# High halves of the weights on GpSimd in the three norm stretches of a layer, on the scalar engine elsewhere

## The chip, the core and the metric

The kernel runs on one core of a Trainium2. Its engines work side by side, each through its own queue in order: TensorE (PE) multiplies, VectorE (DVE), ScalarE (ACT) and GpSimd (POOL) work on elements, and SyncE (SP) starts the transfers between device memory and on-chip memory. A semaphore makes an instruction wait for one of another engine. SBUF is the on-chip memory of operands, PSUM that of TensorE's results. The metric is the time of one execution on the device in microseconds, as the median of three runs, without a profile.

## What is computed

A decoder of two layers, 1024 rows (tokens) of 1024 numbers, all fp32. In each layer the normed rows go through one input projection into three groups of heads, their outputs through an output projection; then a gated MLP with 2816 channels and a short convolution follows. Each of the two parts has a norm before and a norm behind it. Cut to what matters here:

```python
def rms_norm(x, gain, eps=NORM_EPS):
    xf = x.astype(jnp.float32)
    y = xf * lax.rsqrt(jnp.mean(xf * xf, axis=-1, keepdims=True) + eps)
    return (y * gain.astype(jnp.float32)).astype(x.dtype)
...
        h = rms_norm(x, pre_mix_norm[layer])
        proj = h @ w_in[layer]
...
        mix = jnp.concatenate([o_diff, o_dil, o_ssd], axis=-1) @ w_out[layer]
        x = x + rms_norm(mix, post_mix_norm[layer])
        h = rms_norm(x, pre_ffn_norm[layer])
        u = causal_dwconv(h @ ffn_up[layer], ffn_conv_w[layer], ffn_conv_b[layer])
        g, val = jnp.split(u, [D_FF], axis=-1)
        f = (jax.nn.silu(g) * val) @ ffn_down[layer]
        x = x + rms_norm(f, post_ffn_norm[layer])
```

## The kernel before

**Split products.** Every product with weights is made of three products of TensorE in its fast fp32r format. `wsplit` (L139) loads a tile of weights (fp32, buffer `wr`), rounds it to its high half `wh` on ScalarE, and subtracts that on VectorE, which leaves the low half `wl`; both are in line 154:

```python
A.activation(h, r, AF.Copy), V.tensor_tensor(part(lo), r, fr(h), op=ALU.subtract)
```

Activations are split in the same way into `ah` and `al` (or `g`, for the hidden channels). A product adds up wh·ah, wl·ah and wh·al in PSUM: L170, L173 and L174 in `tm3` (rows stand on the partitions, as for the values, the output and the down projection), L230, L233 and L234 in `mm3` (channels stand on the partitions, as for the up projection). `wr` has three buffers, `wh` and `wl` four. A tile of weights has 1024 elements on each of 128 partitions; the last of a down group has 512, those of the values' projection have 768 (two rows of 384) or 2x262.

**Rows and halves.** The 1024 rows are eight tiles of 128, worked on in two halves T=0 and T=1 of four tiles. A half goes through the mixer while the other is in the dense products: `weave` and `follow` take the next step of one Python generator between the steps of another, and a tile scheduler puts each engine's instructions in order by priority and by what they need, and sets the waits. So an edit of one operation can also move its neighbours in the order of an engine.

**A norm.** For each row tile: the square summed along the row on ScalarE (L836 for the output projection, L906 for the down projection, L273 for the second norm, 1.06 us of a row of 1024), mean and constant on VectorE (L113, L117), the power -1/2 on GpSimd (L116, one element on each partition), one step of refinement on VectorE (L119, L120), then row times scale times gain (L308) and the sum with the residual row (L309), both on VectorE. The next layer part's norm follows: square (L273), L113, L117, L116, L119, L120 and the scaled row `P` (L278). TensorE transposes that row (L288, eight squares of 128), ScalarE makes the high half of it (L291) and VectorE the low half (L292).

```python
i = V.tensor_scalar(m[:, :n], ssq, scale, eps, op0=ALU.mult, op1=ALU.add)
...
G.tensor_tensor(r[:, :n], m[:, :n], mhalf[:, :n], op=ALU.pow)
```

**Where a norm is made.** In three stretches of a layer, with dense work laid beside it by `follow`, which gives a number of steps of the dense generator ahead of each transposed row tile:

- A: behind the output projection of half 0 (`out_units(0, pair)`), beside the rest of the values' projection of half 1 (`tm1`, L1012): four tiles of 2x262 and four of 768. The first pair of the up projection (two tiles of 1024) comes behind.
- B: behind the output projection of half 1 (`out_units(1, pair)`), beside the last down group of half 0 (`down_group(0, NG - 1, fT0)`, L1033): tiles of 1024, 512, 1024, 512. VectorE adds each result of it to the sum so far (L884, one input in PSUM). The first pair of the up projection of half 1 comes behind.
- C: in layer 1, beside the values' projection of half 0 (`tm_in(0)`, L995): twelve tiles; the norm is that of the rows which layer 0 ended with.

`up_pair` (L842) makes one pair of the up projection: two tiles of weights, the convolution, the gate (L860, L864). L749 is a scaling on GpSimd in the attention of the mixer, L815 one of VectorE with its input in PSUM. `quiet` and the other names of the change are in the section on it.

Of the kernel before, what the change touches and what calls it, by code (L numbers as in the profile page):

```python
# [13 lines left out]
AF = mybir.ActivationFunctionType  # L14
# [55 lines left out]
def body(ctx, tc, x_in, win, wva, wvb, wvz, wout, wup, wdn, cst, gains, dtb, alog, lamp, kst, rope, out):  # L70
# [34 lines left out]
    def fr(ap):  # L105
        return ap.bitcast(F32)
# [20 lines left out]
    xsrc = [x_in[t] for t in range(8)]  # L127

    ahead = [None, None]
    lastdma = [None]  # L130

    def queue_behind(ins, before):
# [4 lines left out]
    def wsplit(src, step=None):  # L137

        raw = sp.tile([P, KT * P], F32, tag="wr", bufs=3, name="wr")  # L139
        hi = sp.tile([P, KT * P], F32R, tag="wh", bufs=4, name="wh")  # L140
        lo = sp.tile([P, KT * P], F32R, tag="wl", bufs=4, name="wl")
        n = src.shape[-1]
        step = step or n

        def part(t):
            if len(src.shape) == 2:
                return t[:, :n]
            k = src.shape[1]
            if n == step:
                return t[:, :k * n]  # L150
            return t[:, :k * step].rearrange("p (a n) -> p a n", a=k)[:, :, :n]
        r, h = part(raw), part(hi)
        lastdma[0] = Y.dma_start(r if n < step else raw[:, :r.shape[-1]].rearrange("p (a n) -> p a n", n=n) if len(src.shape) == 3 else r, src)
        for i, b in zip((A.activation(h, r, AF.Copy), V.tensor_tensor(part(lo), r, fr(h), op=ALU.subtract)), ahead):  # L154
            if b is not None:
                queue_behind(i, b)
        return hi, lo
# [177 lines left out]
    for l in range(NL):  # L335
# [583 lines left out]
        def ffn(T, pair, fT):  # L919
            for gi, (k0, n) in enumerate(GROUPS):  # L920
                for j in range(k0, k0 + n):
                    yield from up_pair(T, j, pair)
                if gi < len(GROUPS) - 2:
                    yield from down_group(T, gi, fT)

# [10 lines left out]
        if l == 0:  # L936
            hT[0] = act_pair()
            xs = [t4()]
            Y.dma_start(xs[0][:], xsrc[0])
            g0 = sp.tile([P, DM], F32, tag="gb", bufs=2, name="gb")  # L940
            Y.dma_start(g0[:], gains[l, 0])
            Y.dma_start(kc[:, 0:K_TRI], kst[:, 0:K_TRI])
            zero = t2("cv", 4)
            V.memset(zero[:], 0.0)
            wz = tr()
            for _ in range(3):
                T_.matmul(wz[:], zero[:, :P], zero[:], start=True, stop=True)
            rs = [rows() for _ in range(4)]
            done = [pre_a(0, xs[0], rs[0], g0, True)]
            ahead[1] = done[0]  # L950

            def before(t):
                if t == -2:
                    ahead[:] = pre_b(0, rs[0], hT[0])
                if t == -4:
                    xs.extend(load_x(0, 1, 2))
                if t < 0:
                    return
                if t:
                    last = pre_b(t, rs[t], hT[0])  # L960
                if t == 3:
                    done[0] = last[0]
                if t < 3:
                    done.append(pre_a(t + 1, xs[t + 1], rs[t + 1], g0, False, done[t]))
                if t == 0:
                    late[0] = lastdma[0]
                    xs.extend(load_x(0, 2))
                    ahead[:] = None, None
            dense = tm_in(0, before)
            for t in range(4):  # L970
                next(dense)
            load(kc[:, K_TRI:K_MD], kst[:, K_TRI:K_MD])
            gt0 = t2("cv", 4)
            load(gt0[:, :P], kst[:, K_GT:])
            V.tensor_copy(gtr[:, :P], gt0[:, :P])
            cs, sw, fw, sm, nA, nlam = layer_constants()
            for t in range(4):
                next(dense)
            load(kc[:, K_MD:], kst[:, K_MD:K_GT])
            hT[1] = act_pair()  # L980
            xs = load_x(1)
            rs1 = [rows() for _ in range(4)]
            ahead[0] = done[0]
            for t in range(4):
                pre_a(4 + t, xs[t], rs1[t], g0)
            ahead[0] = None
            for t in range(4):
                next(dense, None)
                with tc.high_priority(), tc.issue_after(lastmm[0].ins):
                    pre_b(4 + t, rs1[t], hT[1])  # L990
            run(dense)
        else:
            cs, sw, fw, sm, nA, nlam = layer_constants()
            hT[0] = nextT
            dense = tm_in(0)  # L995
            hT[1] = follow(dense, 1, fin1, (3, 1, 1, 1))
            run(dense)
        dt_sums(0)
        run(units(DILC, (0,)))
        mix0 = chain(attn(0, DILH), attn(0, DIFH))  # L1000
# [8 lines left out]
        run(mix0)  # L1009
        run(dense)  # L1010
        hold[0] = lastmm[0]
        hp = follow(tm1, 0, rs, (0, 1, 1, 1))  # L1012
        run(tm1)
        hold[0] = None
# [15 lines left out]
        dense, rs = out_units(1, pair)  # L1030
        run(dense)
        hold[0] = lastmm[0]
        dense = down_group(0, NG - 1, fT0)  # L1033
        hp = follow(dense, 1, rs, (1, 2, 2, 3))
        run(dense)
# [101 lines left out]
```

## Time and profile before

| what | value |
| --- | --- |
| median of 3 runs | 2664.93 us (2664.46 to 2665.4) |
| time of the profiled execution | 2661.19 us |
| span of the profile | 2659.4 us |
| TensorE busy | 2606.3 us, 98% |
| VectorE busy | 1832.2 us, 69% |
| ScalarE busy | 1246.6 us, 47% |
| GpSimd busy | 229.9 us, 9%, 228 instructions |
| conversions to a high half on ScalarE | 406 instructions, 406.3 us |
| low halves on VectorE | 406 instructions, 477.8 us |
| granted clock of TensorE | 0.996 of full speed |

The span goes from the first to the last instruction in the profile; the profiled execution's own time lies 1.8 us above it, and the median of the runs 3.7 us above that. Busy times are sums over the whole span: a share says how full an engine is on the mean, not where another waits for it. What the span has beside TensorE's busy time is 53.1 us, in which TensorE waits or starts.

### The profile page before, as it was taken

What the parts mean: (1) busy time and instruction counts of PE and PEld (TensorE: products, weight loads), DVE (VectorE), ACT (ScalarE), POOL (GpSimd) and SP (SyncE); (2) the same over time, 40 slices, a digit from 0 to 9 for tenths busy, and PEclk for the clock granted to TensorE, in tenths of its full rate; (3) what the DMA queues carried; (4) which work ended last, traced back from release to release, by engine and by line L of the source; (5) the groups of instructions that cost most, each with busy time, mean ns of one, the idle gap of its engine ahead of it and who ended that gap; (6) DMA issues with size and microseconds to landing.
All of it is one profiled execution on the core that took longest, in us unless ns stands there. A gap on an engine that the chain in (4) does not pass through costs nothing.

```text
span 2659.4 us, 37090 instructions
## 1 busy us (share of the span) xinstructions
PE 2606.3 (98%) x13454; PEld 2160.4 (81%) x13454; DVE 1832.2 (69%) x3855; ACT 1246.6 (47%) x2179; POOL 229.9 (9%) x228
## 2 busy tenths in 40 slices
PE   8999999999999999999999999999999999999998
PEld 7887878887788877888888878788877888788886
DVE  6668856567878586666765688565688775956666
ACT  4465444555534454333344564455565344543332
POOL 0100310110002010000002013101100110100001
PEclk9999999999999999999999999999999999999999
DMA  6654645344433454233257545444434334633332
GB/s 234 220 171 142 209 143 167 115 113 124 139 95 116 122 200 145 95 96 96 88 173 230 162 151 196 144 149 122 121 113 138 97 111 131 233 96 95 97 98 68
DMA packets 163720, 368.92 MB, mean 139 GB/s; under 512 B 18257, under 2 KB 64209, under 8 KB 163537
## 3 DMA queue, kind: packets, MB, share of 16 engines
q1 hardware_dynamic: 163536, 366.54, 44.1%
q8 instruction: 107, 1.75, 0.3%
q14 instruction: 77, 0.62, 0.1%
HBM read 306.18 MB, written 60.29 MB: 138 GB/s over the span
## 4 chain that ended last, share of the span: by engine, by line
PE 80%; DVE 10%; ACT 3%; issue 3%; DMA 2%; POOL 1%; SPq 0%; ACTq 0%; DVEq 0%; POOLq 0%
PE acc L230 16%; PE acc L234 15%; PE acc L233 15%; PE acc L174 7%; PE acc L170 7%; PE acc L173 7%; PE po L781 3%; PE s L631 3%; PE tr L771 3%; DVE wl L154 1%; POOL rs_r L116 1%; DVE cv L395 1%; DVE P L278 1%; DVE P L308 1%; DVE t L309 1%
## 5 line engine op out<-in xcount | busy, mean ns | idle before, releaser
L230 PE MATMUL acc<-ah,wh 128*128 128x512 f32 x1952 | 775.4, 398 | 0.5 <-ACT ah L291 0.5
L234 PE MATMUL acc<-ah,wl 128*128 128x512 f32 x1952 | 764.9, 392 | 0.0
L233 PE MATMUL acc<-al,wh 128*128 128x512 f32 x1952 | 764.5, 392 | 0.0
L154 DVE TENSOR_TENSOR wl<-wr,wh 128x1024 fp32r<-128x1024 f32 (+3 forms) x406 | 477.8, 1182 | 270.6 <-ACT wh L154 263.9
L154 ACT ACTIVATE wh<-wr 128x1024 fp32r<-128x1024 f32 (+3 forms) x406 | 406.3, 1008 | 465.5 <-PE acc L233 262.6
L230 PEld LDWEIGHTS acc<-ah,wh 128*128 128x128 f32 x1952 | 366.6, 188 | 80.5 <-issue 9.3
L234 PEld LDWEIGHTS acc<-ah,wl 128*128 128x128 f32 x1952 | 366.6, 188 | 78.1 <-issue 2.4
L233 PEld LDWEIGHTS acc<-al,wh 128*128 128x128 f32 x1952 | 367.0, 188 | 71.4 <-DVE al L292 0.8
L395 DVE SCALAR_TENSOR_TENSOR cv<-acc,cs,cv 128x511 f32<-128x511 f32 (+2 forms) x436 | 324.5, 744 | 17.8 <-ACT cv L393 15.8
L170 PE MATMUL acc<-wh,g 128*128 128x512 f32 x704 | 280.3, 399 | 3.8 <-DVE cv L401 1.8
L173 PE MATMUL acc<-wl,g 128*128 128x512 f32 x704 | 276.1, 392 | 3.0 <-DVE wl L154 3.0
L174 PE MATMUL acc<-wh,g 128*128 128x512 f32 x704 | 275.7, 394 | 1.6 <-DVE g L864 1.6
L173 PE MATMUL acc<-wl,ah 128*128 128x512 f32 (+2 forms) x640 | 226.0, 354 | 7.1 <-DVE wl L154 6.4
L170 PE MATMUL acc<-wh,ah 128*128 128x512 f32 (+2 forms) x640 | 224.1, 354 | 6.7 <-ACT wh L154 6.2
L636 ACT ACTIVATE P<-P,tiny 128x128 f32<-128x128 f32 (+7 forms) x224 | 173.0, 773 | 115.0 <-DVE tiny L635 109.6
L174 PE MATMUL acc<-wh,al 128*128 128x512 f32 (+2 forms) x640 | 223.7, 351 | 0.4 <-DVE al L292 0.2
L633 DVE CUSTOM_DVE_ANT_0 P<-s,kc 128x512 f32<-128x512 f32 (+3 forms) x224 | 129.7, 588 | 109.0 <-PE s L631 107.5
L116 POOL TENSOR_TENSOR rs_r<-rs_m,kc 128x1 f32<-128x1 f32 (+2 forms) x88 | 71.2, 813 | 1397.8 <-DVE rs L117 1256.2
L170 PEld LDWEIGHTS acc<-wh,g 128*128 128x128 f32 x704 | 132.5, 188 | 38.7 <-ACT g L863 4.3
L393 ACT ACTIVATE cv<-acc,cs 128x512 f32<-128x512 f32 x204 | 155.7, 763 | 13.8 <-PE acc L234 13.3
L174 PEld LDWEIGHTS acc<-wh,g 128*128 128x128 f32 x704 | 132.4, 188 | 32.9 <-DVE g L864 5.6
L173 PEld LDWEIGHTS acc<-wl,g 128*128 128x128 f32 x704 | 132.6, 188 | 29.3 <-DVE wl L154 4.0
(176 smaller groups left out, 3138.3 us busy)
## 6 DMA issues: line engine op xcount, KB each, us to landing
wr<-in_wup SPq DMA_DIRECT2D x176, 512.0 KB, 3.5
wr<-in_wdn SPq DMA_DIRECT2D x80, 512.0 KB, 3.5
wr<-in_win SPq DMA_DIRECT2D x54, 512.0 KB, 5.2
wr<-in_wout SPq DMA_DIRECT2D x32, 512.0 KB, 4.3
xd<-t SPq DMA_DIRECT2D x24, 512.0 KB, 2.6
t<-xd SPq DMA_DIRECT2D x24, 512.0 KB, 3.8
t<-in_x SPq DMA_DIRECT2D x16, 512.0 KB, 4.9
Q<-DQ SPq DMA_DIRECT2D x128, 64.0 KB, 2.0
```

The costliest lines, as they stand in the source:

```text
L116: G.tensor_tensor(r[:, :n], m[:, :n], mhalf[:, :n], op=ALU.pow)
L154: for i, b in zip((A.activation(h, r, AF.Copy), V.tensor_tensor(part(lo), r, fr(h), op=ALU.subtract)), ahead):
L170: i = T_.matmul(a, xh, hi[:, w], start=(n0 + k == 0), stop=False)
L173: T_.matmul(a, xh, lo[:, w], start=False, stop=False)
L174: lastmm[0] = T_.matmul(a, xl, hi[:, w], start=False, stop=(n0 + k == n - 1))
L230: i = T_.matmul(a[:], hi[:, w], xh, start=(k == 0), stop=False)
L233: T_.matmul(a[:], hi[:, w], xl, start=False, stop=False)
L234: i = T_.matmul(a[:], lo[:, w], xh, start=False, stop=(k == nk - 1))
L393: A.activation(u[:], a[:], AF.Identity, scale=w[:, n:n + 1], bias=w[:, taps:taps + 1])
L395: V.scalar_tensor_tensor(u[:, d:], a[:, :H - d], w[:, n - d:n - d + 1], u[:, d:], op0=ALU.mult, op1=ALU.add)
L633: V.tensor_tensor_reduce(p[:, c:c + n], s[:, :n], mask[:, o:o + n], 1.0, -1e30 if c == 0 else mx[:, e], ALU.add, ALU.max, mx[:, e])
L636: A.activation(p[:, :nk * P], p[:, :nk * P], AF.Exp, scale=scale, bias=nm[:, e], accum_out=den[:, e])
```

## The change

A flag `quiet` is set ahead of C, A and B and cleared at the end of C and after the first pair of an `ffn`. While it is set, `wsplit` rounds the high half by a GpSimd instruction (times 1.0 plus 0.0) in place of ScalarE's copy. 44 tiles are moved: 10 in each A (four of 2x262, four of 768, two of 1024), 6 in each B (1024, 512, 1024, 512, 1024, 1024) and 12 in C (four of 768, four of 2x262, four of 768). The low halves stay on VectorE.

```diff
--- before.py
+++ after.py
@@ -127,6 +127,7 @@
     xsrc = [x_in[t] for t in range(8)]
 
     ahead = [None, None]
+    quiet = [False]
     lastdma = [None]
 
     def queue_behind(ins, before):
@@ -151,7 +152,8 @@
             return t[:, :k * step].rearrange("p (a n) -> p a n", a=k)[:, :, :n]
         r, h = part(raw), part(hi)
         lastdma[0] = Y.dma_start(r if n < step else raw[:, :r.shape[-1]].rearrange("p (a n) -> p a n", n=n) if len(src.shape) == 3 else r, src)
-        for i, b in zip((A.activation(h, r, AF.Copy), V.tensor_tensor(part(lo), r, fr(h), op=ALU.subtract)), ahead):
+        up = A.activation(h, r, AF.Copy) if not quiet[0] else G.tensor_scalar(h, r, 1.0, 0.0, op0=ALU.mult, op1=ALU.add)
+        for i, b in zip((up, V.tensor_tensor(part(lo), r, fr(h), op=ALU.subtract)), ahead):
             if b is not None:
                 queue_behind(i, b)
         return hi, lo
@@ -920,6 +922,7 @@
             for gi, (k0, n) in enumerate(GROUPS):
                 for j in range(k0, k0 + n):
                     yield from up_pair(T, j, pair)
+                    quiet[0] = False
                 if gi < len(GROUPS) - 2:
                     yield from down_group(T, gi, fT)
 
@@ -992,9 +995,11 @@
         else:
             cs, sw, fw, sm, nA, nlam = layer_constants()
             hT[0] = nextT
+            quiet[0] = True
             dense = tm_in(0)
             hT[1] = follow(dense, 1, fin1, (3, 1, 1, 1))
             run(dense)
+            quiet[0] = False
         dt_sums(0)
         run(units(DILC, (0,)))
         mix0 = chain(attn(0, DILH), attn(0, DIFH))
@@ -1009,6 +1014,7 @@
         run(mix0)
         run(dense)
         hold[0] = lastmm[0]
+        quiet[0] = True
         hp = follow(tm1, 0, rs, (0, 1, 1, 1))
         run(tm1)
         hold[0] = None
@@ -1030,6 +1036,7 @@
         dense, rs = out_units(1, pair)
         run(dense)
         hold[0] = lastmm[0]
+        quiet[0] = True
         dense = down_group(0, NG - 1, fT0)
         hp = follow(dense, 1, rs, (1, 2, 2, 3))
         run(dense)
```

In the changed kernel every line number is higher by 1 or 2 from L130 on: the conversion is L155, the low half L156, L170/L173/L174 are L172/L175/L176, L278 is L280, L288 is L290, L292 is L294 and L884 is L886; L113 to L120 keep theirs. The scheduler's order moves with the edit. Here are the places that the prediction speaks of.

The queue of GpSimd in B of layer 0 before the change: `rs_r` are the powers, two for each of the four row tiles.

```order
```order
L116 TENSOR_TENSOR rs_r_8960<-rs_m_8959,kc_69 128x1
L116 TENSOR_TENSOR rs_r_8975<-rs_m_8974,kc_69 128x1
L116 TENSOR_TENSOR rs_r_9013<-rs_m_9012,kc_69 128x1
L116 TENSOR_TENSOR rs_r_9028<-rs_m_9027,kc_69 128x1
L116 TENSOR_TENSOR rs_r_9066<-rs_m_9065,kc_69 128x1
L116 TENSOR_TENSOR rs_r_9081<-rs_m_9080,kc_69 128x1
L116 TENSOR_TENSOR rs_r_9119<-rs_m_9118,kc_69 128x1
L116 TENSOR_TENSOR rs_r_9134<-rs_m_9133,kc_69 128x1
```


The same queue after the change, from the second row tile on; `wh` are the high halves.

```order
```order
L116 TENSOR_TENSOR rs_r_9013<-rs_m_9012,kc_69 128x1
L116 TENSOR_TENSOR rs_r_9028<-rs_m_9027,kc_69 128x1
L155 TENSOR_SCALAR wh_9144<-wr_9143 128x1024
L155 TENSOR_SCALAR wh_9150<-wr_9149 128x512
L155 TENSOR_SCALAR wh_9230<-wr_9229 128x1024
L116 TENSOR_TENSOR rs_r_9066<-rs_m_9065,kc_69 128x1
L155 TENSOR_SCALAR wh_9236<-wr_9235 128x512
L116 TENSOR_TENSOR rs_r_9081<-rs_m_9080,kc_69 128x1
L116 TENSOR_TENSOR rs_r_9119<-rs_m_9118,kc_69 128x1
L155 TENSOR_SCALAR wh_9315<-wr_9314 128x1024
L155 TENSOR_SCALAR wh_9355<-wr_9354 128x1024
L116 TENSOR_TENSOR rs_r_9134<-rs_m_9133,kc_69 128x1
```


The six conversions now stand between the powers: three ahead of the first power of the third row tile (`rs_r_9066`), one ahead of its second, two ahead of the last power.

VectorE at the end of B in layer 0, before the change, from the last add of the down group's first results to the low halves of the last normed row tile; `P_8895` is that row, `wl_9316` and `wl_9356` are the low halves of the up projection's first pair.

```order
```order
L884 TENSOR_TENSOR fT_4394<-acc_9266,fT_4394 128x512
L119 SCALAR_TENSOR_TENSOR rs_q_9136<-rs_r_9134,rs_2_9135 128x1
L154 TENSOR_TENSOR wl_9316<-wr_9314,wh_9315 128x1024
L120 SCALAR_TENSOR_TENSOR rs_r_9134<-rs_q_9136,rs_r_9134 128x1
L884 TENSOR_TENSOR fT_4394<-acc_9277,fT_4394 128x512
L278 SCALAR_TENSOR_TENSOR P_8895<-t4_8905,rs_r_9134,gb_8757 128x1024
L884 TENSOR_TENSOR fT_4394<-acc_9288,fT_4394 128x512
L154 TENSOR_TENSOR wl_9356<-wr_9354,wh_9355 128x1024
L292 TENSOR_TENSOR al_9167<-tr_9299,ah_9166 128x4x128
L292 TENSOR_TENSOR al_9167<-tr_9306,ah_9166 128x4x128
```


The same place after the change.

```order
```order
L886 TENSOR_TENSOR fT_4394<-acc_9241,fT_4394 128x512
L119 SCALAR_TENSOR_TENSOR rs_q_9136<-rs_r_9134,rs_2_9135 128x1
L886 TENSOR_TENSOR fT_4394<-acc_9266,fT_4394 128x512
L120 SCALAR_TENSOR_TENSOR rs_r_9134<-rs_q_9136,rs_r_9134 128x1
L156 TENSOR_TENSOR wl_9316<-wr_9314,wh_9315 128x1024
L280 SCALAR_TENSOR_TENSOR P_8895<-t4_8905,rs_r_9134,gb_8757 128x1024
L886 TENSOR_TENSOR fT_4394<-acc_9277,fT_4394 128x512
L886 TENSOR_TENSOR fT_4394<-acc_9288,fT_4394 128x512
L156 TENSOR_TENSOR wl_9356<-wr_9354,wh_9355 128x1024
L294 TENSOR_TENSOR al_9167<-tr_9299,ah_9166 128x4x128
L294 TENSOR_TENSOR al_9167<-tr_9306,ah_9166 128x4x128
```


One L886 has moved from ahead of the scaled row (L280) to behind it, and L120 has moved from behind the first low half to ahead of it.

TensorE at the end of A in layer 0, before the change: `acc_4225` is the last sum of the 2x262 tiles, `tr_4211` and `tr_4218` the last transposed row tile.

```order
```order
L170 MATMUL acc_4225<-wh_4091,ah_547 128x262
L173 MATMUL acc_4225<-wl_4092,ah_547 128x262
L174 MATMUL acc_4225<-wh_4091,al_548 128x262
L288 MATMUL tr_4211<-kc_69,P_3808 128x128 x4
L288 MATMUL tr_4218<-kc_69,P_3808 128x128 x4
L170 MATMUL acc_4278<-wh_4255,ah_547 128x384
```


The same place after the change.

```order
```order
L176 MATMUL acc_4225<-wh_4085,al_548 128x262
L290 MATMUL tr_4211<-kc_69,P_3808 128x128 x4
L290 MATMUL tr_4218<-kc_69,P_3808 128x128 x4
L172 MATMUL acc_4225<-wh_4085,ah_547 128x262
L175 MATMUL acc_4225<-wl_4086,ah_547 128x262
L176 MATMUL acc_4225<-wh_4085,al_548 128x262
L172 MATMUL acc_4225<-wh_4091,ah_547 128x262
L175 MATMUL acc_4225<-wl_4092,ah_547 128x262
L176 MATMUL acc_4225<-wh_4091,al_548 128x262
L172 MATMUL acc_4225<-wh_4091,ah_547 128x262
L175 MATMUL acc_4225<-wl_4092,ah_547 128x262
L176 MATMUL acc_4225<-wh_4091,al_548 128x262
```


Nine products of 262 columns, which stood ahead of the last transposes, now stand behind them.

GpSimd in C, before the change: two powers for each row tile.

```order
```order
L116 TENSOR_TENSOR rs_r_12068<-rs_m_12067,kc_69 128x1
L116 TENSOR_TENSOR rs_r_12083<-rs_m_12082,kc_69 128x1
L116 TENSOR_TENSOR rs_r_12118<-rs_m_12117,kc_69 128x1
L116 TENSOR_TENSOR rs_r_12133<-rs_m_12132,kc_69 128x1
L116 TENSOR_TENSOR rs_r_12168<-rs_m_12167,kc_69 128x1
L116 TENSOR_TENSOR rs_r_12183<-rs_m_12182,kc_69 128x1
```


The same queue after the change, from the third conversion on.

```order
```order
L155 TENSOR_SCALAR wh_12248<-wr_12247 128x768
L116 TENSOR_TENSOR rs_r_12083<-rs_m_12082,kc_69 128x1
L155 TENSOR_SCALAR wh_12254<-wr_12253 128x768
L116 TENSOR_TENSOR rs_r_12118<-rs_m_12117,kc_69 128x1
L155 TENSOR_SCALAR wh_12402<-wr_12401 128x2x262
L116 TENSOR_TENSOR rs_r_12133<-rs_m_12132,kc_69 128x1
L116 TENSOR_TENSOR rs_r_12168<-rs_m_12167,kc_69 128x1
L155 TENSOR_SCALAR wh_12408<-wr_12407 128x2x262
L155 TENSOR_SCALAR wh_12414<-wr_12413 128x2x262
L155 TENSOR_SCALAR wh_12420<-wr_12419 128x2x262
L116 TENSOR_TENSOR rs_r_12183<-rs_m_12182,kc_69 128x1
```


The powers of the second, third and fourth row tile now have conversions ahead of them in the queue, the last of them three of 2x262.

## Rows read from the trace of the kernel before

**Rows 1.** The page, busy time (share), instructions of an engine.
```profile
PE 2606.3 (98%) x13454; PEld 2160.4 (81%) x13454; DVE 1832.2 (69%) x3855; ACT 1246.6 (47%) x2179; POOL 229.9 (9%) x228
```

**Rows 2.** Waits of TensorE: us in total, times, longest.
```profile
PE acc L173 <- DVE wl L154: 9.4, 14, 1.5
...
PE acc L170 <- ACT wh L154: 6.2, 5, 2.1
...
PE tr L288 <- DVE P L278: 6.1, 6, 1.8
```

**Rows 3.** Windows: length, busy us of PE, PEld, DVE, ACT, POOL; clock, DMA.
```profile
389.00:410.00 21.00, 17.26 (x125) 16.16 (x124) 17.06 (x41) 11.14 (x23) 2.62 (x4) 0.92 0.69 210
942.00:965.00 23.00, 21.00 (x99) 17.17 (x99) 21.95 (x44) 12.20 (x20) 3.13 (x4) 0.93 0.63 206
1333.00:1361.00 28.00, 24.90 (x151) 23.53 (x151) 22.97 (x45) 13.71 (x27) 3.90 (x5) 0.99 0.58 187
```

**Rows 4.** Groups by line and form: busy, mean ns.
```profile
L154 ACT ACTIVATE wh<-wr 128x1024 fp32r<-128x1024 f32 x342 | 361.3, 1059 | 418.6 <-PE acc L233 241.3 <-PE acc L174 143.0 <-issue 10.3
...
L749 POOL TENSOR_SCALAR P<-P,tiny 128x1024 f32<-128x1024 f32 x12 | 13.5, 1128 | 75.7 <-DVE tiny L748 75.7
...
L749 POOL TENSOR_SCALAR P<-P,tiny 128x768 f32<-128x768 f32 x12 | 10.9, 911 | 71.6 <-DVE tiny L748 71.6
```

**Rows 5.** Timeline, VectorE and GpSimd at once: start, us, instruction.
```profile
441.71 0.69 DVE L860 TENSOR_TENSOR cv<-cv 128x512 f32<-128x512 f32 x1
...
442.66 0.80 POOL L749 TENSOR_SCALAR P<-P,tiny 128x640 f32<-128x640 f32 x1 [35.61 <-DVE tiny L748]
...
443.10 0.90 DVE L864 TENSOR_TENSOR g<-cv,g 128x512 fp32r<-128x512 f32 x1 [0.63 <-ACT g L863]
...
265.98 3.73 POOL L438 TENSOR_TENSOR g<-g 128x512 fp32r<-128x512 f32 x2 [8.03 <-issue]
...
266.31 2.23 DVE L154 TENSOR_TENSOR wl<-wr,wh 128x1024 fp32r<-128x1024 f32 x1
...
598.54 1.14 POOL L749 TENSOR_SCALAR P<-P,tiny 128x1024 f32<-128x1024 f32 x1 [4.62 <-DVE tiny L748]
...
598.91 0.69 DVE L884 TENSOR_TENSOR fT<-acc,fT 128x512 f32<-128x512 f32 x1 [0.53 <-PE acc L174]
```

**Rows 6.** Timeline of B; in brackets idle before, and releaser.
```profile
940.72 1.29 DVE L278 SCALAR_TENSOR_TENSOR P<-t,rs_r,gb 128x1024 f32<-128x1024 f32 x1
...
942.25 1.22 DVE L154 TENSOR_TENSOR wl<-wr,wh 128x1024 fp32r<-128x1024 f32 x1
...
942.35 1.52 POOL L116 TENSOR_TENSOR rs_r<-rs_m,kc 128x1 f32<-128x1 f32 x1 [2.11 <-DVE rs L117]
...
943.52 0.62 PE L173 MATMUL acc<-wl,g 128*128 128x512 f32 x1 [1.50 <-DVE wl L154]
...
963.25 1.27 DVE L278 SCALAR_TENSOR_TENSOR P<-t,rs_r,gb 128x1024 f32<-128x1024 f32 x1
...
964.67 1.06 PE L288 MATMUL tr<-kc,P 128*128 128x128 f32 x8 [0.50 <-DVE P L278]
...
2286.04 1.06 PE L288 MATMUL tr<-kc,P 128*128 128x128 f32 x8 [1.70 <-DVE P L278]
```

**Rows 7.** Timeline of TensorE in A.
```profile
397.40 0.65 PE L170 MATMUL acc<-wh,ah 128*128 128x262 f32 x2 [2.13 <-ACT wh L154]
...
408.03 0.28 PE L173 MATMUL acc<-wl,ah 128*128 128x262 f32 x1
...
408.15 0.28 PE L174 MATMUL acc<-wh,al 128*128 128x262 f32 x1
...
408.98 1.06 PE L288 MATMUL tr<-kc,P 128*128 128x128 f32 x8 [0.54 <-DVE P L278]
```

**Rows 8.** Timeline of C.
```profile
1349.37 1.00 POOL L116 TENSOR_TENSOR rs_r<-rs_m,kc 128x1 f32<-128x1 f32 x1 [1.91 <-DVE rs L117]
...
1358.20 0.51 PE L170 MATMUL acc<-wh,ah 128*128 128x262 f32 x2 [1.34 <-ACT wh L154]
```

## Prediction

> **What bounds the kernel now.** I read the page first, then the waits of TensorE, then three stretches in order of time. TensorE is busy for 2606.3 of 2659.4 us [rows 1], so a change pays only where it takes away, or adds, a wait of TensorE. The list of its waits names the candidates: 6.2 us on high halves from ScalarE, 9.4 us on low halves from VectorE, 6.1 us on normed rows [rows 2]. By time, the large ones lie in the norm stretches. I call them A (the mixer's output norm while the values of the second half are projected, 383 to 428 in layer 0), B (the same norm of the second half beside the last down group, 934 to 972) and C (the input norm of layer 1, 1322 to 1382); A and B come again in layer 1, so there are five. Next I asked which engine makes TensorE wait there. In the core of A VectorE is busy 17.06 of 21 us and ScalarE 11.14; in B 21.95 of 23 and 12.20; in C 22.97 of 28 and 13.71 [rows 3]. So VectorE, not ScalarE, is the tight engine of all three, and GpSimd is nearly free (2.62, 3.13, 3.90). The reader is to see that B is a chain on VectorE with 1 us of slack in 23.
>
> **What the change does.** 44 high halves move from ScalarE to GpSimd: 10 in each A (4 of 2x262, 4 of 768, 2 of 1024), 6 in each B (1024, 512, 1024, 512, 1024, 1024), 12 in C (4 of 768, 4 of 2x262, 4 of 768). The two of 1024 at the end of A and B belong to the first pair of the up projection. No work is removed, and no transfer is added; those that refill a raw buffer follow its low half as before.
>
> *Their own price.* The form that is added stands in the trace: GpSimd takes 1.128 us for 128x1024 and 0.911 for 128x768 in L749, ScalarE 1.059 for 128x1024 [rows 4]. The slope between the two GpSimd rows is 0.85 ns per element, so 512 and 2x262 come to 0.69 and 0.70. By duration alone 44 moves would be harmless: about 0.07 us each, on an engine with room.
>
> *What they lie on.* A GpSimd instruction that reads SBUF and a VectorE instruction with two SBUF inputs exclude each other. At 442.66 GpSimd runs 0.80 us; L864, which starts at 443.10 and needs 0.69 us alone (as L860 does), takes 0.90 and ends 0.54 after GpSimd does. At 266.31 a low half of 1024 takes 2.23 us instead of its usual 1.22, because GpSimd has a subtraction under way. The other way round, the power at 942.35, 0.55 us otherwise, takes 1.52 us under a low half that began at 942.25. L884, with one input in PSUM, takes 0.69 us beside a GpSimd instruction that runs all the while: it isn't held [rows 5, 6]. In the norm stretches the low halves, L308, L309 and L278 all have two SBUF inputs; only L292, L884 and L815 read PSUM. So a conversion that was beside VectorE's work on ScalarE now stands in its line. And GpSimd works in order: the power of a norm (L116) waits behind a conversion that is queued ahead of it.
>
> No row shows a VectorE instruction of one element per partition (L120, L840) during a long GpSimd instruction. I take it as held, like every larger one with two SBUF inputs; if it isn't, B below gets 0.3 us cheaper. The Trainium skill, in "SBUF — State Buffer", section "Who interferes with whom", says that the pair of ports is an exclusive lock for the whole instruction, whatever its size, and that ScalarE never waits there; the rows on the large instructions agree, and by the rule the sum stays as below. The same skill, in "GPSIMD Engine Reference", section "Engine selection", calls one-input work there roughly line-rate; 1024 elements at 1.2 GHz would be some 0.85 us (an estimate from that page), and the sum would shrink by a quarter; the measured 1.128 decides.
>
> **The sum, by stretches.**
>
> *B, walked through in the first layer [rows 6].* The first conversion starts as soon as the power ahead of it ends, about 940.2, and holds VectorE's L120, and so L278 behind it, for its 1.13 us, until 941.34; L278 starts at 941.4 instead of 940.72, +0.7. When it ends, at 942.7, the second conversion (0.69, of which some is already spent) has waited for the ports and gets them; the first low half ends at 944.3 instead of 943.47, +0.85, and TensorE, which waits 1.50 us for it at 943.52, gets on so much later. The third (1024) has waited meanwhile: 1.0 us more. The second low half ends 1.1 us late, and behind it the third tile's power, which now stands behind that conversion, so that this tile's L308 starts late by that and by the rest of the power that no longer runs under the first low half: +1.95 (an estimate). The fourth falls under PSUM work: 0. The fifth and sixth fall half under L292 and L884: +0.5 at most where they hold L120. ScalarE's relief gives back little, since the waits of VectorE for it are those for the square of a row, whose own 1.06 us stays. That makes the normed row of the last tile (L278 at 963.25, ready 964.52) about 2.3 us late. TensorE already waits for it there, 0.50 us in layer 0 and 1.70 in layer 1, so the lateness is passed on whole. Behind it the new order puts both last L884 and a low half ahead of L292, where one L884 and a low half stood: +0.7 (L884's 0.69) for the first product of the up projection. Together +3.0, twice: **+6.0**. Bounds: 0 if all six fall beside PSUM work, 2 x (1.13 + 0.69 + 1.13) = 5.9 if each is felt.
>
> *A.* Here there is a gain: TensorE waits 2.13 us at 397.40 for a high half that ScalarE gets to late, behind the square of a row [rows 7]. On GpSimd it is ready before 396. But its low half still comes after L308, L292 and L309, which are 1.0 us later by the same holds, so some 1.7 us of earlier low half remain, and the last tile's normed row, for which TensorE waits until 408.98, stays where it is within 0.1. TensorE's new order, though, sets nine products of 2x262 behind the last transposes instead of ahead of them: 9 x 0.12 (408.03 to 408.15) = +1.1 after a wait that TensorE cannot shorten (0.54 at 408.98). Then three conversions of 768 alternate with their low halves (0.91 + 0.81 in turn, where before the two engines overlapped), and the third low half is some 1.0 us late for its product. **+2.0 each, +4.0**. The two of 1024 are started 3 us ahead of need: nothing. Bounds: -2.1 (the wait goes, nothing is held), 4 x 0.69 + 4 x 0.91 = +6.4.
>
> *C.* The first low half is held by two conversions: +1.3. The wait of 1.34 us at 1358.20 [rows 8] for a late high half on ScalarE goes. But from there the powers of the third and fourth tile stand behind conversions which wait for TensorE to free a buffer (the power at 1349.37 is ready to go within 0.1 us of its input; it would start 1 to 3 us later), and the rows that they scale delay the third low half of 2x262 by some 3 us, when TensorE has less other work in hand. Net **+3.0**, the least certain term: -1.5 to +10.0 (8 x 0.91 + 4 x 0.69).
>
> Sum: 6.0 + 4.0 + 3.0 = +13.0 us. The profiled execution took 2661.19 us (span 2659.4), so 2674.2; the runs' median is 3.7 us above the profiled one, hence **2678 us**.
>
> **Rivals.**
> 1. *The waits for ScalarE simply go, the conversions fall beside PSUM work or idle time.* For it: GpSimd idle, 2.13, 2.13 and 1.34 us of waits named. Against it: VectorE's 21.95 of 23 us in B. At most the 6.2 us of the list: 2658.7. It decides if less than a sixth of the conversions' time (34.6 us over the five stretches: 2 x 6.4 + 2 x 5.9 + 10.0) is felt. Chance 0.10.
> 2. *Both cancel*, gains in A and C against B: 2660 to 2670. Chance 0.20.
> 3. *Nearly every conversion is felt, and the powers queue up behind them*: +26 to +35, 2691 to 2700. For it: the in-order queue in C. Against it: in A a third of VectorE's time is idle or PSUM work. Chance 0.10.
> 4. The forecast, +6 to +25: 2671 to 2690. Chance 0.60.
>
> **How the numbers follow.** What a measurement of this kernel can tell from no change is about 0.2%, 5.3 us. Rival 1 is the chance of faster, 0.10; rival 2 of the same, 0.20; forecast and rival 3 together of slower, 0.70. The range runs from the middle of rival 2, 2664, to just inside rival 3, 2692; below and above it lie some 0.2 together.
>
> **What would show it.** In the profile after: GpSimd some 40 us busier; in the five stretches low halves, L308, L309 and L278 (two lines lower there) of 1.5 to 2.3 us where they took 1.2 to 1.3; TensorE's waits for ScalarE's high halves gone, and in their place longer ones for low halves and for the normed row at the end of A and B; B longest per conversion. I am wrong if those VectorE instructions keep their durations, or if they grow and TensorE's waits in the stretches still shrink, as they would if TensorE had more work in hand there than I count.

## The result, and the profile after

The changed kernel takes 2678.43 us (median of 6 runs, 2675.09 to 2680.47), the kernel before 2664.89 (6 runs, 2663.87 to 2665.4): a ratio of 1.0051, 95% interval 1.004 to 1.0062, so 13.5 us more. The forecast was 2678, slower. The profiled execution after has a span of 2675.8 us, 16.4 more than that of before.

The page of the changed kernel, busy time of each engine, as [rows 1]:

```profile
PE 2612.2 (98%) x13454; PEld 2163.9 (81%) x13454; DVE 1848.2 (69%) x3855; ACT 1213.5 (45%) x2135; POOL 271.5 (10%) x272
```

GpSimd is 41.6 us busier, VectorE 16.0. VectorE has the same 3855 instructions as before, so they have become longer. The same three stretches as in [rows 3], moved by what TensorE is late there (columns as there):

```profile
391.00:412.00 21.00, 15.90 (x120) 14.62 (x120) 18.26 (x40) 7.77 (x17) 7.97 (x9) 1.00 0.68 216
...
945.50:970.00 24.50, 21.06 (x96) 17.08 (x95) 23.54 (x43) 8.63 (x16) 6.70 (x9) 0.93 0.53 183
...
1340.00:1369.00 29.00, 25.49 (x149) 23.87 (x147) 24.31 (x45) 10.17 (x20) 10.24 (x13) 0.94 0.53 166
```

VectorE is busy 18.26 of 21, 23.54 of 24.5 and 24.31 of 29 us, GpSimd two to three times what it was (2.62, 3.13, 3.90), and ScalarE over a quarter less. The waits of TensorE, which answer to [rows 2] (us in total, times, longest):

```profile
PE acc L175 <- DVE rs_m L113: 8.9, 4, 3.4
...
PE acc L175 <- DVE wl L156: 7.8, 15, 1.7
...
PE tr L290 <- DVE P L280: 4.6, 6, 1.5
...
PE acc L172 <- POOL wh L155: 4.5, 3, 1.9
...
PE acc L172 <- ACT wh L155: 0.8, 2, 0.6
```

The waits for ScalarE's high halves have shrunk from 6.2 to 0.8 us. In their place stand 4.5 us on GpSimd's, and 8.9 us in four waits of up to 3.4, which the list puts on L113. L113 is a one-element instruction that TensorE never reads; it ends just behind the low half that TensorE does read, and the list names the one that came last. So these are waits for low halves too: 16.7 us together, against 9.4 and 0.7 before.

**Where the time lies.** Both traces have 13,454 products, so the start of the n-th product after, less that of the n-th before, is how late TensorE is. At times of the kernel before, this grows by 2.30 us in A and 2.61 in B of layer 0, 2.19 in C, 3.53 in A and 2.99 in B of layer 1: 13.6 together. Of the other 2.8, 1.5 arise between 300 and 340 and 0.9 between 1620 and 1665, where neither kernel has an edit. The windows of 320 to 330 show why (first the kernel before, then the changed one):

```profile
320.00:330.00 10.00, 9.83 (x64) 9.41 (x64) 6.75 (x17) 6.46 (x17) 3.31 (x4) 1.00 0.35 118
```

```profile
320.00:330.00 10.00, 9.78 (x53) 9.32 (x54) 5.23 (x15) 5.38 (x16) 3.31 (x4) 0.83 0.37 132
```

The granted clock is 1.00 in one and 0.83 in the other, so some of TensorE's products ran at the lower of its two levels. The experiments whose edit comes later (all but copy and fill, nine of eleven) are 1.3 to 5.1 us late at the same place, so it was the profiled execution of before that ran well (2661.19 us, below its median).

### The profile page after: what moved, and what is told of

It reads as the page before. It is cut to its first block, busy times and chain, and to the rows that moved or that the text cites. A ratio compares the mean times of both kernels' runs of the same rounds, so it can differ in the third digit from the quotient of the medians.

```text
span 2675.8 us, 37101 instructions
## 1 busy us (share of the span) xinstructions
PE 2612.2 (98%) x13454; PEld 2163.9 (81%) x13454; DVE 1848.2 (69%) x3855; ACT 1213.5 (45%) x2135; POOL 271.5 (10%) x272
## 5 line engine op out<-in xcount | busy, mean ns | idle before, releaser
L156 DVE TENSOR_TENSOR wl<-wr,wh 128x1024 fp32r<-128x1024 f32 (+3 forms) x406 | 483.3, 1196 | 267.4 <-ACT wh L155 256.1
L155 ACT ACTIVATE wh<-wr 128x1024 fp32r<-128x1024 f32 (+3 forms) x362 | 371.6, 1030 | 449.8 <-PE acc L235 258.5
L172 PE MATMUL acc<-wh,g 128*128 128x512 f32 x704 | 280.5, 399 | 4.9 <-DVE fT L886 2.5
L175 PE MATMUL acc<-wl,g 128*128 128x512 f32 x704 | 276.2, 392 | 6.7 <-DVE rs_m L113 6.7
L176 PE MATMUL acc<-wh,g 128*128 128x512 f32 x704 | 275.5, 393 | 1.6 <-DVE g L866 1.6
L175 PE MATMUL acc<-wl,ah 128*128 128x512 f32 (+2 forms) x640 | 226.8, 355 | 10.1 <-DVE wl L156 7.8
L172 PE MATMUL acc<-wh,ah 128*128 128x512 f32 (+2 forms) x640 | 227.1, 357 | 7.7 <-POOL wh L155 4.5
L176 PE MATMUL acc<-wh,al 128*128 128x512 f32 (+2 forms) x640 | 225.1, 353 | 0.4 <-DVE al L294 0.2
L116 POOL TENSOR_TENSOR rs_r<-rs_m,kc 128x1 f32<-128x1 f32 (+2 forms) x88 | 71.5, 816 | 1359.6 <-DVE rs L117 1218.3
L172 PEld LDWEIGHTS acc<-wh,g 128*128 128x128 f32 x704 | 132.4, 188 | 40.3 <-ACT g L865 4.4
L175 PEld LDWEIGHTS acc<-wl,g 128*128 128x128 f32 x704 | 132.5, 188 | 33.0 <-DVE wl L156 3.8
L176 PEld LDWEIGHTS acc<-wh,g 128*128 128x128 f32 x704 | 132.4, 188 | 32.7 <-DVE g L866 5.6
```

What stands on the lines that cost most here:

```text
L155: up = A.activation(h, r, AF.Copy) if not quiet[0] else G.tensor_scalar(h, r, 1.0, 0.0, op0=ALU.mult, op1=ALU.add)
L156: for i, b in zip((up, V.tensor_tensor(part(lo), r, fr(h), op=ALU.subtract)), ahead):
L172: i = T_.matmul(a, xh, hi[:, w], start=(n0 + k == 0), stop=False)
L175: T_.matmul(a, xh, lo[:, w], start=False, stop=False)
L176: lastmm[0] = T_.matmul(a, xl, hi[:, w], start=False, stop=(n0 + k == n - 1))
```

## The experiments

Each was timed beside the kernel before on its chip. "Late" is TensorE's progress against the trace of before, over one stretch (383 to 428, 934 to 972 and 1322 to 1382 of before, in layer 1 1700 to 1750 and 2255 to 2300). The same stretches in experiments that don't touch them are late by -0.8 to 0.7 us (A, layer 0), 0.6 to 2.8 (A, layer 1), -0.4 to 0.2 (B) and -1.5 to 0.1 (C). So B can be read to 0.4 us. In A and C the spread goes with the granted clock of the stretch; here C in before and in only_b, which doesn't touch it (columns as in [rows 3]):

```profile
1322.00:1382.00 60.00, 56.59 (x334) 52.86 (x333) 42.61 (x97) 26.21 (x47) 5.55 (x8) 0.97 0.50 167
```

```profile
1328.00:1386.00 58.00, 54.58 (x332) 50.92 (x331) 42.02 (x97) 26.12 (x47) 5.55 (x8) 1.00 0.52 172
```

At 0.97, as in before, the three untouched C are 0.0 to 0.1 late; at 1.00 the two others are 1.5 early. A of layer 0 has 0.96 in before: the untouched are 0.6 and 0.7 late at 0.96, and 0.8 early at 1.00. A of layer 1 has 1.00 in before: the untouched are 0.6 to 1.9 late at 0.97 and 2.8 at 0.94. So A and C are to be compared at one clock, which the table gives. "Hold" is the sum over VectorE's instructions that overlap a GpSimd instruction of the edit, of what their duration has above the median of the same form in that trace.

| run | ratio, interval | late: A, A | late: B, B | late: C | clock: A, A, C | hold |
| --- | --- | --- | --- | --- | --- | --- |
| the change | 1.0051 (1.0040 to 1.0062) | 2.30, 3.53 | 2.61, 2.99 | 2.19 | 1.00, 0.97, 0.97 | 17.2 |
| only_a | 1.0021 (1.0011 to 1.0031) | 2.34, 3.09 | not touched | not touched | 1.00, 1.00, - | 7.3 |
| only_b | 1.0021 (1.0011 to 1.0030) | not touched | 2.51, 3.09 | not touched | - | 5.4 |
| only_c | 1.0010 (1.0001 to 1.0019) | not touched | not touched | 2.14 | -, -, 0.97 | 4.4 |
| copy | 1.0043 (1.0031 to 1.0056) | 1.30, 1.45 | 3.01, 4.13 | 1.45 | 0.96, 1.00, 0.97 | 6.7 |
| half | 1.0018 (1.0009 to 1.0027) | 1.79, 1.91 | 1.95, 1.13 | -0.60 | 0.96, 0.97, 1.00 | 6.2 |
| fill | 1.0009 (1.0000 to 1.0018) | 0.56, 2.63 | -0.20, 1.37 | -1.63 | 0.96, 0.94, 1.00 | |
| b456 | 1.0008 (0.9999 to 1.0017) | not touched | 0.73, 1.16 | not touched | - | 2.2 |
| b1 | 1.0007 (0.9998 to 1.0016) | not touched | 0.43, 0.81 | not touched | - | 1.6 |
| a4 | 1.0002 (0.9993 to 1.0010) | 0.97, 1.56 | not touched | not touched | 1.00, 1.00, - | 3.1 |
| prio | 1.0008 (1.0000 to 1.0017) | -0.39, 0.37 | 3.67, 5.05 | -1.17 | 1.00, 1.00, 0.97 | |
| prio_ac | 0.9987 (0.9978 to 0.9996) | 1.05, 0.37 | not touched | -1.12 | 1.00, 1.00, 0.97 | |

**One stretch at a time.** In the three kernels the flag is set in one of the places only; for only_a:

```diff
-            quiet[0] = True
+            quiet[0] = False
             dense = tm_in(0)
...
-        quiet[0] = True
+        quiet[0] = False
         dense = down_group(0, NG - 1, fT0)
```

> The conversions of A alone are on GpSimd, those of B and C on ScalarE. Theory (a GpSimd conversion holds VectorE, and TensorE waits for what is late): A keeps its own loss, 2.0 us in layer 0 and about 3 in layer 1 by TensorE's progress in the changed kernel, so +4 to +6 on the kernel before, and TensorE's progress through B and C is that of before. Rival (the loss is not in the stretches, but in the scheduler's other order or the clock elsewhere): under +2, or over +8.

> The conversions of B alone are on GpSimd. Theory: +3.1 us in each B, so +6 (5 to 7.5), of which about 2.4 stand at the first scaled row (L280), held by three conversions in a row. Rival (six conversions fall beside PSUM work): 0 to +2.

> The conversions of C alone are on GpSimd. Theory: +2.3 us by TensorE's progress in the changed kernel (1 to 4), half of it at the first low half and 1.3 at the last three conversions, which alternate with their low halves. Rival (powers of the norm stand behind conversions in GpSimd's queue): over +4, with powers that start more than 1 us after their input.

Times of +6.0, +6.6 and +2.4 us (medians 2670.8, 2671.32 and 2667.12 against 2664.77), 14.9 together against 13.5 for the whole change: the loss is in the stretches, and adds up. Each stretch is late by what it is in the changed kernel, to within 0.5 us.

**Copies that nobody reads.** The conversions go back to ScalarE, and GpSimd copies the raw tile:

```diff
-        up = A.activation(h, r, AF.Copy) if not quiet[0] else G.tensor_scalar(h, r, 1.0, 0.0, op0=ALU.mult, op1=ALU.add)
+        up = A.activation(h, r, AF.Copy)
+        if quiet[0]:
+            G.tensor_scalar(part(sp.tile([P, 8, P], F32, tag="vv", bufs=1, name="xx").rearrange("p k n -> p (k n)")), r, 1.0, 0.0, op0=ALU.mult, op1=ALU.add)
```

> The conversions are all on ScalarE, as before; in the three stretches GpSimd copies the same raw tiles into a tile that nobody reads, 44 copies that nothing waits for. Theory (the hold of VectorE alone costs the time): VectorE's L280, L310 and low halves grow as in the changed kernel, and the time is +6 to +14 on before. Rival (a conversion that comes late itself, or the new order, costs the time): within 2 us of before.

The time came out as the theory had it (+12.5 us, median of five from 2673.03 to 2678.11; the trace is of the fastest), the reason did not. In B, where most of it lies, the copies of the first three tiles ran long before the norm, and nothing is held at its start; GpSimd and VectorE at the start of B, then TensorE's wait (start, us, instruction, in brackets idle before):

```profile
942.04 1.06 POOL L116 TENSOR_TENSOR rs_r<-rs_m,kc 128x1 f32<-128x1 f32 x2 [4.54 <-DVE rs L117]
...
950.14 0.62 POOL L157 TENSOR_SCALAR xx<-wr 128x512 f32<-128x512 f32 x1 [7.03 <-DMA wr<-in_wdn]
...
943.47 1.28 DVE L282 SCALAR_TENSOR_TENSOR P<-t,rs_r,gb 128x1024 f32<-128x1024 f32 x1
...
944.66 1.28 DVE L312 SCALAR_TENSOR_TENSOR P<-P,rs_r,gb 128x1024 f32<-128x1024 f32 x1
...
945.86 1.22 DVE L158 TENSOR_TENSOR wl<-wr,wh 128x1024 fp32r<-128x1024 f32 x1
...
947.13 0.50 PE L177 MATMUL acc<-wl,g 128*128 128x512 f32 x1 [3.62 <-DVE wl L158]
```

The scheduler has put both scaled rows (L282, L312) ahead of the first low half, where one stood ahead before, and TensorE waits 3.62 us for that low half, against 1.50 [rows 6]. So a new order alone can cost as much as the change does in B. The run does not tell hold from order. In the changed kernel itself TensorE's order in both B is that of before, and VectorE's too up to the end of L280, so what L280 is late there is hold; further experiments follow.

**Half of the columns.** GpSimd converts the second half of each tile, ScalarE the first:

```diff
...
+        else:
+            m = r.shape[1] // 2
+            A.activation(h[:, :m], r[:, :m], AF.Copy)
+            up = G.tensor_scalar(h[:, m:], r[:, m:], 1.0, 0.0, op0=ALU.mult, op1=ALU.add)
```

> Of each of the 44 tiles GpSimd converts one half of the columns and ScalarE the other, so that each hold is about half as long. Theory (the length of the hold is what VectorE loses): about half of the changed kernel's loss, +5 to +9 on before. Rival (what costs is that GpSimd gets to a conversion late, its queue, or the other order of instructions): +11 or more, as for whole tiles.

+4.4 us (2669.36 against 2665.00), a third of the change's loss and a little under what was expected; its hold, too, is about a third (6.2 of 17.2). At the start of B the three conversions take 1.58 us together instead of 2.64, and L285, which is L280 of the changed kernel, takes 1.61 us instead of 2.04:

```profile
943.70 1.58 POOL L160 TENSOR_SCALAR wh<-wr 128x512 fp32r<-128x512 f32 x3
...
944.73 1.61 DVE L285 SCALAR_TENSOR_TENSOR P<-t,rs_r,gb 128x1024 f32<-128x1024 f32 x1
```

**Writes without reads.** As in copy, but with `G.memset(..., 0.0)` of the same shapes.

> The conversions are on ScalarE; in the stretches GpSimd fills a tile that nobody reads with zeros, 44 times, in the shapes of the tiles of weights: instructions that write SBUF and read nothing. Theory in its narrow form (the hold comes from a GpSimd instruction that reads SBUF): within 2 us of before, and VectorE's instructions keep their durations. In its wide form (any GpSimd instruction with an operand in SBUF holds VectorE): +8 to +13, as the copies did.

+2.4 us, between the two forms and nearer to the narrow one. But the fills, which wait for nothing in the stretches, ran ahead of them. Those of A stand ahead of a power (128x8) in GpSimd's queue, and TensorE waits 1.71 us at 294.11 and 1.70 at 1617.02 for L719, which needs that power; before it did not wait there. In A and C it is as late as the untouched ones at the same clock. GpSimd and VectorE at 288 us, where five fills of 0.5 and 0.7 us follow one another from 287.50 on:

```profile
287.50 3.52 POOL L157 MEMSET xx<- 128x524 f32 x5
...
288.75 0.95 DVE L158 TENSOR_TENSOR wl<-wr,wh 128x768 fp32r<-128x768 f32 x1
...
289.61 0.64 DVE L113 TENSOR_SCALAR rs_m<-tiny 128x8 f32<-128x8 f32 x1
```

A low half beside them takes 0.95 us, its usual time (median 0.951); low halves of 1024 beside fills at 755.77 and 763.47 take 1.22. That agrees with the Trainium skill, "SBUF — State Buffer", section "Who interferes with whom": two SBUF inputs contend with a GpSimd instruction that reads SBUF, not with one that only writes. L113, with one SBUF input and eight elements per partition, does take 0.64 us instead of 0.17; the same section of the Trainium skill lists `tensor_scalar` among the instructions that can take both ports in a fast mode, which would explain it, and no run here tests that further.

**A few conversions at a time.** In the first kernel GpSimd converts the fourth to sixth tile of each B, in the second the first alone, in the third the four of 2x262 of each A; a count in `quiet` replaces the flag, for b456:

```diff
+        up = A.activation(h, r, AF.Copy) if quiet[0] != 1 else G.tensor_scalar(h, r, 1.0, 0.0, op0=ALU.mult, op1=ALU.add)
+        quiet[0] -= quiet[0] > 1
...
-        quiet[0] = True
+        quiet[0] = 4
         dense = down_group(0, NG - 1, fT0)
```

> GpSimd converts three tiles in each B, the fourth to the sixth, which in the changed kernel lie beside VectorE's work from PSUM; the first three, which it converted in a row, and A and C are on ScalarE. Theory (a conversion costs where VectorE has two-input work from SBUF ready): 0 to +1.5 in all. Rival (every conversion costs alike): half of B's loss, +3.

> GpSimd converts only the first tile of each B; everything else is on ScalarE. Theory (the hold of VectorE is the loss, and three conversions in a row hold L280 for the sum of their times): one conversion of 1024 holds L119 or L120 for about 1.0 us, so the first low half ends 0.8 to 1.0 us late and B loses 0.5 to 1.0 each by TensorE's progress, against 2.5 and 3.1 with all six. Rival (the loss comes from the order, or from GpSimd's powers behind conversions, not from the time of the hold): as with all six, or nothing.

> GpSimd converts only the four tiles of 2x262 of each A; the four of 768 and two of 1024 behind them are on ScalarE again. Theory (the last three conversions of 768 alternate with their low halves, +1.1 us of A's loss): A loses 1.0 to 1.3 us less than with all ten, so about +1 in layer 0 and +2 in layer 1 by TensorE's progress. Rival (nine products moved behind the last transposes make the end of A's loss): as with all ten.

The times are +2.8, +1.7 and +0.5 us, none clear of no change, so TensorE's progress has to tell. In b456 and b1 the order on TensorE is that of before, in b456 on VectorE too, so that what b456 loses is hold. In b1, where one low half has moved on VectorE, it can be followed step by step: the conversion, the held L119 (0.22 us otherwise), L281, and TensorE's wait:

```profile
942.38 1.05 POOL L155 TENSOR_SCALAR wh<-wr 128x1024 fp32r<-128x1024 f32 x1
...
942.43 1.00 DVE L119 SCALAR_TENSOR_TENSOR rs_q<-rs_r,rs 128x1 f32<-128x1 f32 x1 [0.60 <-POOL rs_r L116]
...
943.66 1.28 DVE L281 SCALAR_TENSOR_TENSOR P<-t,rs_r,gb 128x1024 f32<-128x1024 f32 x1
...
946.21 0.50 PE L176 MATMUL acc<-wl,g 128*128 128x512 f32 x1 [2.23 <-DVE rs_m L113]
```

0.78 us of hold, 0.73 more of TensorE's wait (2.23 against 1.50), 0.43 and 0.81 late. In b456 the hold falls on L120 and L311 (L308 of before) at the end of B:

```profile
959.78 2.07 POOL L155 TENSOR_SCALAR wh<-wr 128x1024 fp32r<-128x1024 f32 x2 [3.13 <-PE acc L177]
...
959.90 0.94 DVE L120 SCALAR_TENSOR_TENSOR rs_r<-rs_q,rs_r 128x1 f32<-128x1 f32 x1
...
961.36 1.56 DVE L311 SCALAR_TENSOR_TENSOR P<-P,rs_r,gb 128x1024 f32<-128x1024 f32 x1
```

1.1 us of hold here, 0.73 late, and 1.9 late over both layers, more than the 0 to 1.5 expected: beside PSUM work there was L120, and one-element instructions are held as long as large ones. a4 gives back 1.4 and 1.5 us of A's loss at the same clock (2.34 and 3.09 with all ten), a little more than the 1.0 to 1.3 expected. Its order in A is that of the changed kernel on VectorE, and on TensorE but for one product, the nine products behind the transposes included: what it gives back belongs to the conversions of 768, not to the order, and the rival falls.

**Conversions first on ScalarE.** No GpSimd at all; conversion and low half at high priority while `quiet` is set, in prio_ac not in B:

```diff
+        with (tc.high_priority() if quiet[0] else ExitStack()):
+            up = A.activation(h, r, AF.Copy)
+            dn = V.tensor_tensor(part(lo), r, fr(h), op=ALU.subtract)
```

> All conversions on ScalarE, but conversion and low half are emitted at high priority in the three stretches, so that the fourth tile of 2x262 stands ahead of the square of a row on ScalarE, and the low half ahead of the next norm's work on VectorE. If ScalarE's late conversion was a fault of order (TensorE's waits of 2.13, 2.13 and 1.34 us in before), 2 to 5 us less than before. Rival: the low halves push the normed rows back on VectorE, which is full there: 0 to +4.

> All conversions on ScalarE; conversion and low half emitted at high priority in A and C, but not in B, where this cost 3.7 and 5.1 us. From TensorE's progress with high priority in all three (A about 0, C 1.2 us ahead of before, where the same stretches without any edit stood 0.6 to 2 us behind it): 1 to 4 us less than before. Rival (ScalarE's late conversion is replaced by a normed row that is late): within 1 us of before or slower.

With B in it, B loses 3.7 and 5.1 us and the whole is slower by 0.08%. Without it, 0.9987 of before (2662.53 against 2664.81 us): the fastest version here, and the only one clear of no change on that side. TensorE's wait for a high half in A, 2.13 us at 397.40 [rows 7], is 0.73 there:

```profile
398.51 0.64 ACT L156 ACTIVATE wh<-wr 128x524 fp32r<-128x524 f32 x1 [3.15 <-DMA wr<-in_wvb]
...
400.01 1.06 ACT L277 ACTIVATE P<-t 128x1024 f32<-128x1024 f32 x1 [0.86 <-DVE tiny L844]
...
399.20 0.39 PE L174 MATMUL acc<-wh,ah 128*128 128x262 f32 x1 [0.73 <-ACT wh L156]
```

The conversion now stands ahead of the row's square. That the 2.3 us come from there is not shown: at the same clock prio and prio_ac are 0.4 to 1.8 us late in A, and 1.2 ahead in C. The profiled execution of prio_ac, 2664.77, lies 2.2 above its median.

## Why the prediction held, step by step

*VectorE is tight, not ScalarE.* Right: 33 us less work on ScalarE gave nothing that outweighs the holds, and prio_ac, which moves no work off ScalarE, is 2.3 us faster than before.

*The exclusion.* Right. The start of B after, GpSimd then VectorE, with [rows 6] for before:

```profile
944.21 2.64 POOL L155 TENSOR_SCALAR wh<-wr 128x1024 fp32r<-128x1024 f32 x3
...
949.27 0.98 POOL L116 TENSOR_TENSOR rs_r<-rs_m,kc 128x1 f32<-128x1 f32 x1 [2.42 <-DVE rs L117]
...
944.26 1.00 DVE L119 SCALAR_TENSOR_TENSOR rs_q<-rs_r,rs 128x1 f32<-128x1 f32 x1 [0.60 <-POOL rs_r L116]
...
945.29 0.55 DVE L120 SCALAR_TENSOR_TENSOR rs_r<-rs_q,rs_r 128x1 f32<-128x1 f32 x1
...
945.88 2.04 DVE L280 SCALAR_TENSOR_TENSOR P<-t,rs_r,gb 128x1024 f32<-128x1024 f32 x1
...
947.91 1.21 DVE L156 TENSOR_TENSOR wl<-wr,wh 128x1024 fp32r<-128x1024 f32 x1
...
951.75 1.28 DVE L310 SCALAR_TENSOR_TENSOR P<-P,rs_r,gb 128x1024 f32<-128x1024 f32 x1
...
949.18 0.50 PE L175 MATMUL acc<-wl,g 128*128 128x512 f32 x1 [3.37 <-DVE rs_m L113]
...
970.68 1.06 PE L290 MATMUL tr<-kc,P 128*128 128x128 f32 x8 [0.76 <-DVE P L280]
```

Three conversions take 2.64 us in a row; L119 ends with the first of them, L120 with the second, L280 takes 2.04 us instead of 1.29. The open point, whether a one-element instruction with two SBUF inputs is held, is settled: 1.00 us instead of 0.22. The form's own price, 1.128 us from L749, was a little high: an unheld conversion of 1024 takes 1.04 to 1.06, the row of 1.119 is a mean with one that was held and took 1.91:

```profile
L155 POOL TENSOR_SCALAR wh<-wr 128x1024 fp32r<-128x1024 f32 x12 | 13.3, 1119 | 24.1 <-PE acc L176 24.1
```

*B, +3.0 each.* Measured 2.61 and 2.99. TensorE is 4.0 us late when B begins; with that taken off, L280 starts 1.16 us late (0.7 was forecast) and ends 1.91 late, the first low half ends 1.65 late (0.85), the third tile's L310 1.90 (951.75 against 945.85; 1.95), the last L280 2.00 (2.3), the transposes behind it 2.01, and TensorE is 2.6 late at the end (the forecast's +0.7 for the order behind L280 is there with 0.6). The sum held and one step did not: I let the second and third conversion take turns with VectorE's work. GpSimd's next conversion starts 0.03 us ahead of the end of the one before, and L119, L120 and L280 were held by one each (0.78, 0.39 and 0.75 us), so nearly all the loss fell at once: TensorE waits 3.37 us for the first low half, against 1.50. The low half itself was not held. The wait for the last normed row, at which the forecast had the rest of the lateness appear, did not take it (0.76 against 0.50; in layer 1 0.97 against 1.70), since TensorE was late already. The bound of 5.9 us for both B counts three of the six conversions of each; with all six it is 11.8.

*A, +2.0 each.* Late by 2.30 and 3.53. At one clock it is 3.1 in layer 0 (the untouched are 0.8 early there) and, by only_a, 3.1 in layer 1 against before alone; only_a's +6.0 us agrees. The term was too small, because a loss at the start was missing: the first two conversions hold L119 and L120 here too (0.57 us at 388.76, 0.56 at 389.37), in VectorE's order of before. TensorE waits 1.10 us at 391.99 for the first low half, where it waited 0.35, and is 1.1 late behind it in each A that has these conversions whole, and within 0.1 of before in the untouched. The gain was there and smaller than I said: the fourth high half was to be ready before 396, but its data landed at 396.84 (395.5 in times of before), and the conversion took 1.68 us, held under L311.

```profile
396.84 1.68 POOL L155 TENSOR_SCALAR wh<-wr 128x524 fp32r<-128x524 f32 x1 [3.16 <-DMA wr<-in_wvb]
...
408.71 2.50 POOL L155 TENSOR_SCALAR wh<-wr 128x768 fp32r<-128x768 f32 x2 [0.76 <-PE acc L176]
...
411.44 1.26 POOL L155 TENSOR_SCALAR wh<-wr 128x768 fp32r<-128x768 f32 x1 [0.24 <-POOL wh L155]
...
396.82 1.22 DVE L311 TENSOR_TENSOR t<-t,P 128x1024 f32<-128x1024 f32 x1
...
410.44 3.06 DVE L156 TENSOR_TENSOR wl<-wr,wh 128x768 fp32r<-128x768 f32 x2 [0.73 <-POOL wh L155]
...
398.57 0.39 PE L172 MATMUL acc<-wh,ah 128*128 128x262 f32 x1 [1.91 <-POOL wh L155]
...
409.86 1.06 PE L290 MATMUL tr<-kc,P 128*128 128x128 f32 x8 [0.23 <-DVE P L280]
...
413.56 0.44 PE L175 MATMUL acc<-wl,ah 128*128 128x384 f32 x1 [0.18 <-DVE wl L156]
...
415.69 0.44 PE L175 MATMUL acc<-wl,ah 128*128 128x384 f32 x1 [0.80 <-DVE wl L156]
```

TensorE waits 1.91 us for it, against 2.13. What was lost at the end came about as forecast, 1.3 us for 1.0: the conversions of 768 and their low halves in turn (two low halves take 3.06 us instead of 1.9), and waits of 0.18 and 0.80 us for them. The nine products behind the transposes are in a4 too, which is 0.97 late, 1.7 at one clock. Without the 1.1 at the start, 0.6 is left for them and for everything else in the middle of A, where 1.1 was forecast for them alone; they were not tried by themselves.

*C, +3.0.* Late by 2.19, at a clock at which the untouched are 0.0 to 0.1 late. The start came as forecast: conversions hold L119 and L120, in the order of before on TensorE and VectorE, and with the 6.73 us taken off that TensorE is late when C begins, the first low half (before, then after) starts 1.25 late (1.3):

```profile
1334.72 0.95 DVE L154 TENSOR_TENSOR wl<-wr,wh 128x768 fp32r<-128x768 f32 x1
```

```profile
1342.70 0.95 DVE L156 TENSOR_TENSOR wl<-wr,wh 128x768 fp32r<-128x768 f32 x1
```

The largest term did not: the powers were not 1 to 3 us late behind conversions.

```profile
1339.27 2.43 POOL L155 TENSOR_SCALAR wh<-wr 128x768 fp32r<-128x768 f32 x3
...
1355.53 0.63 POOL L155 TENSOR_SCALAR wh<-wr 128x524 fp32r<-128x524 f32 x1 [5.59 <-PE acc L176]
...
1356.13 0.55 POOL L116 TENSOR_TENSOR rs_r<-rs_m,kc 128x1 f32<-128x1 f32 x1
...
1357.76 1.58 POOL L116 TENSOR_TENSOR rs_r<-rs_m,kc 128x1 f32<-128x1 f32 x1 [1.08 <-DVE rs L117]
...
1376.85 3.13 POOL L155 TENSOR_SCALAR wh<-wr 128x768 fp32r<-128x768 f32 x3 [9.80 <-PE acc L176]
```

One power (1356.13) waited 0.3 us for a conversion, which TensorE had kept waiting for a buffer; the others started within 0.1 us of their input. Three take 1.25 to 1.58 us, under low halves and scaled rows; before it was two, with 1.25 and 1.00. At the start three conversions ran in a row (1339.27, as in B), and at the end came the alternation of 768 that I had counted in A and forgotten in C (1376.85, 3.13 us): TensorE's waits there are 1.4 us together, against 0.3. The wait for the late high half on ScalarE went, as forecast.

*The sum.* At one clock the stretches make 6.2 (A), 5.6 (B) and 2.2 (C), where 4.0, 6.0 and 3.0 were forecast. The mechanism was right; that the sum of 13.0 lies so near to the measured 13.5 is in part luck, since A was too low and B and C too high.

*The rivals.* The first (nothing is felt) and the second (both cancel) fall with only_a and only_b, both over 0.1% slower. The third fails because 42 us of conversions made 17.2 us of hold, and TensorE is 13.6 late.

## What to carry to other kernels

Before work is moved to GpSimd, look at what VectorE does in the same microseconds, not at how idle GpSimd is: a GpSimd instruction that reads SBUF costs VectorE up to its whole duration when VectorE has an instruction with two SBUF inputs ready, down to one element per partition, and several in a row add up (1.92 us of hold from 2.64 us of conversions at the start of B). Count the small instructions of a chain too: beside work from PSUM, where a conversion looked free, it held a one-element step of the norm. If an instruction comes late on an engine that isn't full, try its place in that engine's queue too: here that gained 2.3 us in A and C together and lost in B, where another engine lost 13.5.

## What was not expected of the hardware

A run of conversions is not interleaved with VectorE's waiting instruction of 1024 (2.64 us for three; only the one-element instructions end between them). Executions of the same code differ by up to 5.1 us at one place far from any edit, where the granted clock was 1.00, 0.83 or 0.66 between 320 and 330 us (before, after, only_b), so changes of a few us are to be read by stretch, and at one clock: the same C is 1.5 us shorter at 1.00 than at 0.97.
